# Broadcasts by a repeated column, one-product running maximum, and 30 instead of 24 diagonal taps in a two-block kernel

## The chip, the cores and the metric

The kernel runs as one program on one core of one Trainium2 chip. Its engines are TensorE (PE in the profile; PEld is its weight load), VectorE (DVE), ScalarE (ACT), GpSimd (POOL) and SyncE (SP), which here only issues transfers. The metric is the device time of one execution in microseconds, the median of several.

## The reference

Two decoder blocks run one after the other on 512 tokens of 1024 features, all in float32. Three parts of the reference matter here.

- Every block starts and many end with an RMS norm: a factor per token, `rsqrt(mean(x*x) + eps)`, that multiplies all features of that token.
- The first block's mixer has a stabilised mLSTM. With `b` the running sum of the log forget gates and `i` the input gates, `m` is a running maximum over the tokens, and the weights are `exp(b_t - b_s + i_s - m_t)`. There are four heads and two directions, so eight such units.
- The second block's mixer has a causal depthwise convolution of 31 taps over 512 channels: `cv[t, c] = sum_j w[j, c] * gl[t + j - 30, c] + b[c]`. Behind it stand a layer norm over the channels, a SiLU and an output projection:

```
    gl = glu_a * jax.nn.sigmoid(glu_b)
    cv = causal_dwconv(gl, dw_w) + dw_b
    yb = jax.nn.silu(layernorm(cv, ln_g, ln_b))
    return jnp.concatenate([ya, yb], axis=-1) @ w_out
```

## The kernel before, in words

Activations lie feature-major: 128 features on the partitions, 512 tokens along the row. Weight matrices come in 512 KB pieces (`ws`); ScalarE writes the rounded high part (`wh`, line 208), VectorE the rest (`wl`, line 209), and TensorE makes three products of the float32r type for each pair (lines 237 to 239). An fp32 operand that isn't split goes through TensorE in two passes, which the profile shows as two matmul records for one instruction. The stages follow each other: `mix1` (mLSTM and a gated linear attention), `ffn1`, `pool` (the mixer with the 31 taps), `xa0` (attention to a memory), `ffn2a`, `mla`, `xa1`, `ffn2b`, `final`. Key and value projections of the memory (`mem_kv`) are independent work, which is put between other work as a filler of TensorE.

The order of the instructions on each engine is set when the program is built: the code emits them in program order, with priorities for some, and a list scheduler with its own cost estimates orders each engine's queue. Each queue then runs strictly in that order. `pin` keeps the taps of the convolution in the order in which the code emits them.

Three places matter.

**Per-token factors.** `bcast_cols` (lines 312 to 326) gets a column of 128 factors for each of four token groups and must put them on all partitions as rows. For each group VectorE scales the identity by the column (`dg`, two buffers), and TensorE multiplies ones by that matrix (line 318). ScalarE copies the result out of PSUM as `rb`, or the consumer reads PSUM directly. It is called 13 times.

**Running maximum.** `mx` holds the maxima of the four heads, on partitions 0 to 3 for the forward and 64 to 67 for the backward direction. `ml_build` (one call for each of the eight units) spreads one row of it over all partitions with an fp32 product whose stationary operand is a repeated column of the identity (line 907). ScalarE makes the exponentials from it (line 921) and VectorE multiplies them with the scores (line 926). The PSUM banks in this stage are two each for the tags `mm`, `st`, `nd` and `aux`. The spread maxima lie in `aux`, as do the gate products of the gated linear attention (line 986).

**The 31 taps.** The 512 channels are four groups c of 128. Tap 0 starts the sum `c2` on ScalarE. The other 30 taps of a group are dealt out three ways: `POOLC[c]` taps are products on ScalarE (line 1294, tile `cm`) that GpSimd adds into `c2` (line 1295); `PEC[c]` taps are products of a diagonal matrix, built by ScalarE (line 1272, tile `dgc`), with the shifted rows on TensorE (line 1279), summed in PSUM; VectorE does what is left by a fused multiply and add into the same PSUM bank (line 1303), and then adds both sums as `cv` (line 1307). With `POOLC = (9, 8, 5, 3)` and `PEC = (0, 8, 8, 8)` VectorE has 21, 14, 17 and 19 taps. As each `cv` is ready, TensorE adds it into the mean over the channels (line 1368). `ORDER` lists what the mixer's TensorE work is (`a`, `b` the gated halves, `p` the pooled part, `w` its weights, `k` a piece of `mem_kv`); after each entry eight steps of the tap generator are emitted, and a step is a tap that is not a diagonal one. When the list is done, the rest of the taps and of `mem_kv` alternate. Then come the layer norm's sums (line 1419), the factors, and the output projection.

Of the kernel before, what the change touches and what calls it, by code (L numbers as in the profile page):

```python
# [10 lines left out]
F32 = mybir.dt.float32  # L11
F32R = mybir.dt.float32r
U8 = mybir.dt.uint8
I32 = mybir.dt.int32
ACTF = mybir.ActivationFunctionType
ALU = mybir.AluOpType
# [3 lines left out]
P = 128  # L20
S = 512
# [2 lines left out]
DEC = (3, 6)  # L24
LAG = 0
POOLC = (9, 8, 5, 3)
PEC = (0, 8, 8, 8)
ORDER = 'a1 p3 b2 k a2 p2 k b3 a3 p1 k p0 w3 k w2 w1 w0'
KVS = (0, 2, 0, 1)
TURN = (((2,), (0,)), ((1, 3),))  # L30
# [32 lines left out]
def kernel(ctx: ExitStack, tc: tile.TileContext, A, out, stages=ALL_STAGES):  # L63
    nc = tc.nc
    V, SC, GP, PE, DMA = nc.vector, nc.scalar, nc.gpsimd, nc.tensor, nc.sync
# [20 lines left out]
    def pm(tag="mm", shape=(P, S)):  # L86
        n = used[tag] = used.get(tag, -1) + 1
        b = banks[tag][n % len(banks[tag])]
        return psp.tile(list(shape), F32, tag=f"b{b}", bufs=1, name=tag)

    def ptmp(shape=(P, S), dtype=F32, tag="t", bufs=6):
        return tp.tile(list(shape), dtype, tag=tag, bufs=bufs, name=tag)
# [11 lines left out]
    ident = const.tile([P, P], F32, name="ident")  # L104
    ones = const.tile([P, P], F32, name="ones")
# [71 lines left out]
    def pc(name, i=0):  # L177
        c = base[name] + i
        return par[:, c:c + 1]
# [121 lines left out]
    def rsqrt_mean(src, dim, m):  # L301

        v = col(m)
        V.tensor_scalar(out=v, in0=src, scalar1=1.0 / dim, scalar2=EPS, op0=ALU.mult, op1=ALU.add)
        y, t = col(m), col(m)
        GP.tensor_tensor(out=y, in0=v, in1=mhalf[:, 0:m], op=ALU.pow)
        V.scalar_tensor_tensor(out=t, in0=y, scalar=-0.5, in1=y, op0=ALU.mult, op1=ALU.mult)
        V.tensor_tensor(out=t, in0=t, in1=v, op=ALU.mult)
        V.scalar_tensor_tensor(out=y, in0=t, scalar=1.5, in1=y, op0=ALU.add, op1=ALU.mult)
        return y  # L310

    def bcast_cols(r, m=4, pool=None, stay=False):

        ps = pm("aux", (P, m * P))
        for j in range(m):
            dg = ptmp((P, P), tag="dg", bufs=2)
            V.tensor_scalar(out=dg, in0=ident, scalar1=r[:, j:j + 1], scalar2=None, op0=ALU.mult)
            PE.matmul(ps[:, j * P:(j + 1) * P], lhsT=ones, rhs=dg, start=True, stop=True)  # L318
        if stay:
            return ps  # L320
        if pool is None:
            rb = ptmp((P, m * P), tag="rb", bufs=2)
        else:
            rb = pool.tile([P, m * P], F32, tag="rbp", name="rbp")
        SC.activation(out=rb, in_=ps, func=ACTF.Copy)
        return rb

    class Norm:
# [29 lines left out]
        def finish(self, r=None):  # L358
            if self.g is None:
                return None  # L360
            self.r = self.ss.rstd(D) if r is None else r
            if not self.final:
                self.rb = bcast_cols(self.r)
            return self
# [294 lines left out]
    def mix_heads(mp, layers):  # L659
# [19 lines left out]
        with nc.allow_non_contiguous_dma(reason="a column of 128 for each of 8 feature tiles"):  # L679
            (SC, DMA, GP)[LQ].dma_start(out=par[:, base["mix_pre"]:base["mix_pre"] + KD],  # L680
                         in_=A["norm_mix_pre"].rearrange("o (z p) -> p (o z)", p=P))
# [7 lines left out]
                      in_=wi[:, g0:g0 + 16].rearrange("(k p) c -> p k c", p=P))  # L689
        DMA.dma_start(out=wst[:, :, 16:48],  # L690
                      in_=wi[:, l0:l0 + 32].rearrange("(k p) c -> p k c", p=P))
# [36 lines left out]
        ps = opened[1][0]  # L728
# [6 lines left out]
        def log_sigmoid(dst, x, t):  # L735
# [11 lines left out]

        bt = ptmp()
        um = ptmp()
        mx = mp.tile([P, S], F32, name="mx")  # L750
        GP.memset(um, 0.0)
        GP.memset(mx, 0.0)
        bo = one.to_broadcast([P, S])
# [1 line left out]
                             op0=ALU.mult, op1=ALU.add)  # L755
# [5 lines left out]
                             op0=ALU.mult, op1=ALU.max)  # L761
        V.tensor_tensor_scan(out=mx[64:68, ::-1], data0=bo[32:36], data1=um[32:36, ::-1],
                             initial=0.0, op0=ALU.mult, op1=ALU.max)
        V.tensor_tensor(out=um[64:68], in0=bt[0:4], in1=mx[0:4], op=ALU.add)
        V.tensor_tensor(out=um[96:100], in0=bt[64:68], in1=mx[64:68], op=ALU.add)
        ps = pm("aux")
# [4 lines left out]
        for d in range(2):  # L771
            V.tensor_copy(umc[:, :, 4 * d:4 * d + 4], psv[:, :, 32 * d:32 * d + 4])
            SC.activation(out=em[:, :, 4 * d:4 * d + 4], in_=psv[:, :, 64 + 32 * d:68 + 32 * d],
                          func=ACTF.Exp, scale=-1.0)
# [52 lines left out]
        def w5(nm_, shape=(P, 2, S)):  # L827
            return mp.tile(list(shape), F32, tag="w5", bufs=3, name=nm_)
# [71 lines left out]
        def span(d, j):  # L900
            return (j * P, S) if d == 0 else (0, (j + 1) * P)

        def ml_build(h, d):
            q, k2 = qs[h], khl[h]
            mb = pm("aux")
            r0 = 64 * d + h
            PE.matmul(mb, lhsT=ident[:, r0:r0 + 1].to_broadcast([P, P]), rhs=mx, start=True,
                      stop=True)
            e = w5("e", (P, 1280))
            for js in GRP[d]:  # L910
                st = pm("st")
                o0 = OFF[d][js[0]]
                tot = 0
                for j in js:
                    a, b = span(d, j)
                    o = OFF[d][j] - o0
                    ks = slice(j * P, (j + 1) * P)
                    for i in range(2):
                        PE.matmul(st[:, o:o + b - a], lhsT=k2[:, i, ks], rhs=q[:, a:b],
                                  start=i == 0, stop=i == 1)  # L920
                    SC.activation(out=e[:, OFF[d][j]:OFF[d][j] + b - a], in_=mb[:, a:b],
                                  func=ACTF.Exp, scale=-1.0,
                                  bias=umc[:, j, 4 * d + h:4 * d + h + 1])
                    tot += b - a
                sl = slice(o0, o0 + tot)
                V.tensor_tensor(out=e[:, sl], in0=st[:, :tot], in1=e[:, sl], op=ALU.mult)
                for j in js:
                    a, b = span(d, j)
                    o = OFF[d][j] + (0 if d == 0 else b - a - P)
                    sg = 1 if d == 0 else -1  # L930
                    GP.affine_select(out=e[:, o:o + P], in_=e[:, o:o + P], pattern=[[sg, P]],
                                     compare_op=ALU.is_ge, fill=0.0, base=0,
                                     channel_multiplier=-sg)
            return e
# [300 lines left out]
    def pool_mix(nm, nxt, pp, fill):  # L1235
# [29 lines left out]
        own = {c: {1 + i * 30 // POOLC[c] for i in range(POOLC[c])} for c in range(4)}  # L1265
        dia = {c: [j for j in range(1, 31) if j not in own[c]][:PEC[c]] for c in range(4)}

        def diagonals(c):
            dgs[c] = []
            for j in dia[c]:  # L1270
                dg = pp.tile([P, P], F32, tag="dgc", bufs=10, name="dgc")
                SC.activation(out=dg, in_=ident, func=ACTF.Copy, scale=pc("dw_w", 4 * j + c))
                dgs[c].append(dg)

        def conv_pe(c):
            gl = gls[c]
            cps[c] = pm("cv")
            for n, j in enumerate(dia[c]):
                PE.matmul(cps[c], lhsT=dgs[c][n], rhs=gl[:, j:j + S], start=n == 0,
                          stop=n == PEC[c] - 1)  # L1280

        pin = tc.keep_in_program_order

        def conv(c):
            gl, ps = gls[c], cps[c]
            c2 = pp.tile([P, S], F32, tag="c2", bufs=2, name="c2")
            SC.activation(out=c2, in_=gl[:, 0:S], func=ACTF.Identity, scale=pc("dw_w", c),
                          bias=pc("dw_b", c))
            fresh = not PEC[c]
            for j in range(1, 31):  # L1290
                w = pc("dw_w", 4 * j + c)
                if j in own[c]:
                    t = pp.tile([P, S], F32, tag="cm", bufs=4, name="cm")
                    pin(SC.activation(out=t, in_=gl[:, j:j + S], func=ACTF.Copy, scale=w))
                    pin(GP.tensor_tensor(out=c2, in0=c2, in1=t, op=ALU.add))
                elif j in dia[c]:
                    continue
                elif fresh:
                    V.tensor_scalar(out=ps, in0=gl[:, j:j + S], scalar1=w, scalar2=None,
                                    op0=ALU.mult)  # L1300
                    fresh = False
                else:
                    pin(V.scalar_tensor_tensor(out=ps, in0=gl[:, j:j + S], scalar=w, in1=ps,  # L1303
                                               op0=ALU.mult, op1=ALU.add))
                yield
            cv = pp.tile([P, S], F32, name=f"cv{c}")
            V.tensor_tensor(out=cv, in0=ps, in1=c2, op=ALU.add)
            cvs[c] = cv
            yield
# [104 lines left out]
        for c in range(4):  # L1414
            V.tensor_tensor(out=cvs[c], in0=cvs[c], in1=mean, op=ALU.subtract)
            sq = ptmp(tag="sq", bufs=3)
            SC.activation(out=sq, in_=cvs[c], func=ACTF.Square)
            for j in range(4):
                PE.matmul(pss[:, j:j + 1], lhsT=sq[:, j * P:(j + 1) * P], rhs=ones[:, 0:1],
                          start=c == 0 and j == 0, stop=c == 3 and j == 3)  # L1420
# [10 lines left out]
        r = rsqrt_mean(pss, S, 4)  # L1431
# [3 lines left out]
        for c in range(4):  # L1435
            V.scalar_tensor_tensor(out=cvs[c], in0=cvs[c], scalar=pc("ln_g", c), in1=lb,
                                   op0=ALU.mult, op1=ALU.mult)
# [383 lines left out]
    pcs, pp = ExitStack(), []  # L1821
# [78 lines left out]
```

## Time and profile before

| | |
|---|---|
| median of three runs | 2183.96 us (2183.51 to 2189.16) |
| the profiled execution | 2181.3 us, of which the span of the trace is 2178.9 us |
| mean granted TensorE clock | 0.989 of full speed |
| TensorE busy | 2105.1 us (97%) |
| VectorE busy | 1208.9 us (55%) |
| ScalarE busy | 945.9 us (43%) |
| GpSimd busy | 372.7 us (17%) |

Busy is the share of the span in which an engine executes something. Matmuls overlap each other, so TensorE's work is read from the distance between starts, not from the duration of one. In a row of the timeline the first number is the start in us, the second the duration, and the bracket at the end the idle time of that engine just before, with what ended it. PEclk is the TensorE clock that was granted in a stretch, as a share of full speed (2.4 GHz; the lower level is 1.2 GHz).

### The profile page before, as it was taken

How to read it: one execution, taken by the hardware profiler on the slowest of the kernel's cores; microseconds unless marked ns; L12 is line 12 of the kernel's file. 1: busy time of each engine (PE TensorE's matmuls, PEld its weight loads, DVE VectorE, ACT ScalarE, POOL GpSimd, SP SyncE). 2: the span in 40 equal slices, each digit the busy share in tenths (PEclk: the TensorE clock that was granted, in tenths of full speed). 3: DMA queues.
4: the chain of work that ended last, by engine and by line, in shares of the span. 5: the costliest groups of instructions: out<-in, count | busy, mean ns of one | idle time of the engine just before them, and what ended most of it. 6: DMA issues, size and time to landing. Idle time of an engine off the chain costs nothing.

```text
span 2178.9 us, 27908 instructions
## 1 busy us (share of the span) xinstructions
PE 2105.1 (97%) x10807; PEld 1768.7 (81%) x10807; DVE 1208.9 (55%) x1795; ACT 945.9 (43%) x1561; POOL 372.7 (17%) x414
## 2 busy tenths in 40 slices
PE   7999899999999999899999999999999999999998
PEld 6888778788888876778888888888888888888887
DVE  6655755655532378755665554337885565555432
ACT  5765554433332454343443333226774343333322
POOL 2113411211100047020111110112322011111010
PEclk9999999999999999999999999999999999999999
DMA  5543245233333332532233333331124223333331
GB/s 144 161 152 114 88 145 165 73 102 97 97 112 98 114 102 82 174 118 77 73 92 97 97 97 96 116 107 45 35 93 151 78 58 87 97 97 97 94 102 66
DMA packets 369984, 222.88 MB, mean 102 GB/s; under 512 B 22407, under 2 KB 351036, under 8 KB 369852
## 3 DMA queue, kind: packets, MB, share of 16 engines
q1 hardware_dynamic: 366304, 219.65, 33.9%
q8 instruction: 85, 1.39, 0.3%
q10 hardware_dynamic: 3228, 1.42, 0.2%
q14 instruction: 47, 0.39, 0.1%
q0 software_dynamic: 320, 0.04, 0.0%
HBM read 201.41 MB, written 19.66 MB: 101 GB/s over the span
## 4 chain that ended last, share of the span: by engine, by line
PE 80%; DVE 8%; ACT 5%; issue 3%; POOL 1%; DMA 1%; SPq 0%; ACTq 0%; POOLq 0%; DVEq 0%
PE mm L239 21%; PE mm L237 21%; PE mm L238 21%; PE st L237 2%; PE st L238 2%; PE st L239 2%; PE nd L237 2%; PE nd L238 2%; PE nd L239 1%; DVE wl L209 1%; ACT wh L208 1%; DVE cv L1303 1%; ACT pr L1727 1%; PE aux L318 1%; DVE c L1726 1%
## 5 line engine op out<-in xcount | busy, mean ns | idle before, releaser
L208 ACT ACTIVATE wh<-ws 128x1024 fp32r<-128x1024 f32 (+2 forms) x352 | 361.3, 1029 | 774.1 <-PE mm L239 556.7
L209 DVE TENSOR_TENSOR wl<-ws,wh 128x1024 fp32r<-128x1024 f32 (+2 forms) x352 | 421.9, 1200 | 335.7 <-ACT wh L208 335.4
L237 PE MATMUL mm<-a,wh 128*128 128x512 f32 (+1 forms) x1364 | 530.2, 389 | 2.8 <-ACT a L208 1.3
L239 PE MATMUL mm<-a,wh 128*128 128x512 f32 (+1 forms) x1364 | 528.1, 387 | 1.6 <-DVE a L215 1.6
L238 PE MATMUL mm<-a,wl 128*128 128x512 f32 (+1 forms) x1364 | 527.9, 387 | 0.8 <-DVE wl L209 0.8
L237 PEld LDWEIGHTS mm<-a,wh 128*128 128x128 f32 x1364 | 258.4, 190 | 54.7 <-ACT a L208 1.7
L239 PEld LDWEIGHTS mm<-a,wh 128*128 128x128 f32 x1364 | 258.2, 189 | 54.0 <-DVE a L215 3.4
L238 PEld LDWEIGHTS mm<-a,wl 128*128 128x128 f32 x1364 | 258.3, 189 | 51.6 <-DVE wl L209 2.0
L237 PE MATMUL mm<-hh,wh 128*128 128x512 f32 (+1 forms) x550 | 209.6, 381 | 0.0
L238 PE MATMUL mm<-hh,wl 128*128 128x512 f32 (+1 forms) x550 | 209.3, 381 | 0.0
L239 PE MATMUL mm<-hl,wh 128*128 128x512 f32 (+1 forms) x550 | 209.3, 381 | 0.0
L283 POOL TENSOR_TENSOR sq<-sq 128x512 f32<-128x512 f32 x60 | 92.4, 1540 | 646.6 <-ACT sq L278 562.0
L1203 POOL TENSOR_TENSOR t<-t,rb 128x512 f32<-128x512 f32 x66 | 85.1, 1290 | 613.9 <-ACT t L1202 613.9
L1190 DVE TENSOR_TENSOR t<-mm,rb 128x512 f32<-128x512 f32 x64 | 44.2, 691 | 147.2 <-PE mm L239 147.2
L1206 DVE TENSOR_TENSOR t<-mm,t 128x512 f32<-128x512 f32 x65 | 45.0, 692 | 140.4 <-POOL t L1203 140.4
L239 PEld LDWEIGHTS mm<-hl,wh 128*128 128x128 f32 x550 | 103.4, 188 | 19.8
L238 PEld LDWEIGHTS mm<-hh,wl 128*128 128x128 f32 x550 | 103.4, 188 | 19.7
L237 PEld LDWEIGHTS mm<-hh,wh 128*128 128x128 f32 x550 | 103.4, 188 | 19.6
L237 PE MATMUL mm<-wh,a 128*128 128x256 f32 x346 | 100.1, 290 | 2.3 <-DVE Kl L209 2.3
L239 PE MATMUL mm<-wl,a 128*128 128x256 f32 x346 | 99.6, 288 | 1.8 <-DVE wl L209 1.7
L1199 DVE SCALAR_TENSOR_TENSOR t<-t,par 128x511 f32<-128x511 f32 (+1 forms) x132 | 98.7, 748 | 3.2 <-ACT t L1195 0.9
L1202 ACT ACTIVATE t<-t 128x512 f32<-128x512 f32 x66 | 41.7, 632 | 133.6 <-DVE t L1199 133.5
(469 smaller groups left out, 3553.3 us busy)
## 6 DMA issues: line engine op xcount, KB each, us to landing
ws<-in_ffn_w_up_dram SPq DMA_DIRECT2D x110, 512.0 KB, 3.8
ws<-in_ffn_w_down_dram SPq DMA_DIRECT2D x48, 512.0 KB, 3.8
ws<-in_xa_wkv_dram SPq DMA_DIRECT2D x32, 512.0 KB, 4.4
ws<-in_w_in_dram SPq DMA_DIRECT2D x24, 512.0 KB, 5.0
ws<-in_ffn_w_gate_dram SPq DMA_DIRECT2D x22, 512.0 KB
ws<-in_ffn_w_down_dram SPq DMA_DIRECT2D x24, 384.0 KB, 3.4
ws<-in_xa_wq_dram SPq DMA_DIRECT2D x16, 512.0 KB, 5.5
ws<-in_xa_wo_dram SPq DMA_DIRECT2D x16, 512.0 KB, 3.7
```

Of the source, the lines that this page charges most:

```text
L208: SC.activation(out=hi, in_=src, func=ACTF.Copy)
L209: eng.tensor_tensor(out=lo, in0=src, in1=hi.bitcast(F32), op=ALU.subtract)
L237: PE.matmul(ps, lhsT=lh, rhs=rh, start=start, stop=False)
L238: PE.matmul(ps, lhsT=ll, rhs=rh, start=False, stop=False)
L239: PE.matmul(ps, lhsT=lh, rhs=rl, start=False, stop=stop)
L283: GP.tensor_tensor(out=self.acc, in0=self.acc, in1=self.new, op=ALU.add)
L318: PE.matmul(ps[:, j * P:(j + 1) * P], lhsT=ones, rhs=dg, start=True, stop=True)
L1190: V.tensor_tensor(out=g, in0=pg, in1=rb, op=ALU.mult)
L1199: V.scalar_tensor_tensor(out=cv[:, o], in0=g[:, i], scalar=w, in1=cv[:, o], op0=ALU.mult, op1=ALU.add)
L1202: SC.activation(out=ge, in_=cv, func=func)
L1203: GP.tensor_tensor(out=ge, in0=ge, in1=rb, op=ALU.mult)
L1206: V.tensor_tensor(out=h, in0=pu, in1=ge, op=ALU.mult)
```

## The change

- `bcast_cols` makes no scaled identity any more: the stationary operand of the product is the column of factors itself, repeated 128 times by a step of zero, and the moving operand is the identity. Four VectorE instructions a call go.
- The running maxima are put into a float32r tile `mhl` once: the rounded part on their own partitions, the rest 32 partitions further on. A selecting matrix `sel` (the sum of two columns of the identity) then spreads both with one float32r product for each unit.
- `PEC` is (0, 9, 10, 11): 30 diagonal taps in place of 24, and VectorE has 21, 13, 15 and 16. The ring of diagonals has 11 buffers in place of 10. The tap products between ScalarE and GpSimd go through eight tiles (five `cm` and three of the ring `sq`) in place of four.

```
-PEC = (0, 8, 8, 8)
+PEC = (0, 9, 10, 11)
@@ bcast_cols
         for j in range(m):
-            dg = ptmp((P, P), tag="dg", bufs=2)
-            V.tensor_scalar(out=dg, in0=ident, scalar1=r[:, j:j + 1], scalar2=None, op0=ALU.mult)
-            PE.matmul(ps[:, j * P:(j + 1) * P], lhsT=ones, rhs=dg, start=True, stop=True)
+            PE.matmul(ps[:, j * P:(j + 1) * P], lhsT=r[:, j:j + 1].to_broadcast([P, P]), rhs=ident,
+                      start=True, stop=True)
@@ mix_heads
-        mx = mp.tile([P, S], F32, name="mx")
+        mx = ptmp()
+        mhl = mp.tile([P, S], F32R, name="mx")
+        sel = ptmp((P, P), F32R, tag="dg", bufs=2)
...
+        SC.activation(out=mhl, in_=mx, func=ACTF.Copy)
+        for r0 in (0, 64):
+            V.tensor_tensor(out=mhl[r0 + 32:r0 + 36], in0=mx[r0:r0 + 4],
+                            in1=mhl[r0:r0 + 4].bitcast(F32), op=ALU.subtract)
+        V.tensor_tensor(out=sel[:, 0:96], in0=ident[:, 0:96], in1=ident[:, 32:P], op=ALU.add)
@@ ml_build
-            PE.matmul(mb, lhsT=ident[:, r0:r0 + 1].to_broadcast([P, P]), rhs=mx, start=True,
+            PE.matmul(mb, lhsT=sel[:, r0:r0 + 1].to_broadcast([P, P]), rhs=mhl, start=True,
                       stop=True)
@@ pool_mix
-                dg = pp.tile([P, P], F32, tag="dgc", bufs=10, name="dgc")
+                dg = pp.tile([P, P], F32, tag="dgc", bufs=11, name="dgc")
...
+        def tap_tiles():
+            while True:
+                for n in range(8):
+                    yield ptmp(tag="sq", bufs=3) if n % 3 == 2 or n == 7 else \
+                        pp.tile([P, S], F32, tag="cm", bufs=5, name="cm")
...
-                    t = pp.tile([P, S], F32, tag="cm", bufs=4, name="cm")
+                    t = next(cms)
```

The scheduler places the instructions anew, and the order moves at these places. The lines of the change count from its own code: 1368 of before is 1384 there, 1419 is 1435, 907 is 914, 919 is 926, 943 is 950, 986 is 993, 318 is 316.

First TensorE at the end of the taps, before: the product of the last group's `cv` with ones stands behind the filler (the 256-column products), and ahead of the pooled part's product (`ph`, `pl`) and the layer norm's sums.

```order
L239 MATMUL mm<-wl,a 128x256
L1368 MATMUL aux<-cv_7720,ones 128x512
L237 MATMUL mm<-ph,wh 128x512
L238 MATMUL mm<-ph,wl 128x512
L239 MATMUL mm<-pl,wh 128x512
L1419 MATMUL aux<-ones,sq 128x1 x4
L237 MATMUL mm<-a,wh 128x512
```

The same place of the change:

```order
L237 MATMUL mm<-ph,wh 128x512
L238 MATMUL mm<-ph,wl 128x512
L239 MATMUL mm<-pl,wh 128x512
L1384 MATMUL aux<-cv_7684,ones 128x512
L237 MATMUL mm<-wh,a 128x256
L238 MATMUL mm<-wh,a 128x256
L239 MATMUL mm<-wl,a 128x256
```

48 filler products of 256 columns now stand between the last `cv` and the first sums (line 1435), where before there were three products. In the same way the third group's `cv` now stands ahead of 28 such products that were ahead of it before.

Second TensorE in the mLSTM, at the third head, before: `mx` is spread for a unit, its scores follow (`qs`, `khl`), then `mx` for the next unit, and then 48 filler products (`mhl` here is a memory operand).

```order
L943 MATMUL nd<-v,e 128x130 x2
L907 MATMUL aux<-mx,ident 128x512
L919 MATMUL st<-qs_833,khl 128x512 x2
L919 MATMUL st<-qs_833,khl 128x384 x2
L919 MATMUL st<-qs_833,khl 128x128 x2
L907 MATMUL aux<-mx,ident 128x512
L237 MATMUL nd<-mhl,wh 128x256
L238 MATMUL nd<-mhl,wl 128x256
L239 MATMUL nd<-mhl,wh 128x256
```

The same place of the change (its `mx` is the new float32r tile, `dg` the selecting matrix):

```order
L926 MATMUL st<-qs_831,khl 128x256 x2
L914 MATMUL aux<-mx,dg 128x512 x2
L926 MATMUL st<-qs_831,khl 128x512 x2
L926 MATMUL st<-qs_831,khl 128x384 x2
L926 MATMUL st<-qs_831,khl 128x128 x2
L993 MATMUL aux<-sm,w_333 128x512
L926 MATMUL st<-qs_831,khl 128x256 x2
L237 MATMUL nd<-mhl,wh 128x256
```

A gate product (line 993), which needs an `aux` bank, and the unit's last scores have moved ahead of the 48 filler products.

Third TensorE at the factors in front of the pool stage, before: two products of a scaled identity (`dg`), then filler, then the other two.

```order
L239 MATMUL mm<-a,wh 128x256
L318 MATMUL aux<-dg,ones 128x128 x2
L237 MATMUL mm<-a,wh 128x256
L238 MATMUL mm<-a,wl 128x256
L318 MATMUL aux<-dg,ones 128x128 x2
L239 MATMUL mm<-a,wh 128x256
```

The same place of the change, where the moving operand is `ident` and the repeated column `c` is stationary:

```order
L239 MATMUL mm<-a,wh 128x256
L316 MATMUL aux<-ident,c 128x128 x4
L237 MATMUL mm<-a,wh 128x256
L238 MATMUL mm<-a,wl 128x256
L239 MATMUL mm<-a,wh 128x256
```

The four products stand together where the first pair stood.

## Rows read from the trace of the kernel before

**Rows 1.** The page: busy time, share of the span, instructions of each engine.

```profile
PE 2105.1 (97%) x10807; PEld 1768.7 (81%) x10807; DVE 1208.9 (55%) x1795; ACT 945.9 (43%) x1561; POOL 372.7 (17%) x414
```

**Rows 2.** Waits of TensorE: total us, times, longest us.

```profile
PE aux L318 <- DVE dg L317: 3.5, 6, 1.0
```

**Rows 3.** Stretches of 10 us: length, busy times, granted clock, DMA share, GB/s.

```profile
830.00:840.00 10.00, 6.97 (x13) 2.84 (x12) 9.86 (x14) 4.08 (x9) 6.67 (x8) 0.83 0.32 105
900.00:910.00 10.00, 6.75 (x37) 4.99 (x35) 8.28 (x12) 3.62 (x5) 0.00 (x0) 0.85 0.60 177
910.00:920.00 10.00, 7.21 (x28) 6.02 (x27) 5.42 (x10) 4.86 (x9) 0.00 (x0) 0.67 0.71 236
920.00:930.00 10.00, 9.54 (x52) 7.83 (x50) 3.97 (x12) 2.93 (x4) 1.02 (x1) 0.96 0.38 137
```

**Rows 4.** Timeline of TensorE around the first group of diagonal products.

```profile
802.39 0.39 PE L239 MATMUL mm<-nl,wh 128*128 128x512 f32 x1
802.62 7.03 PE L1279 MATMUL cv<-gl,dgc 128*128 128x512 f32 x16
...
809.72 0.39 PE L238 MATMUL mm<-nh,wl 128*128 128x512 f32 x1
```

**Rows 5.** Tile mx: ns min/median/max, first and last start, forms.

```profile
L907 PEld LDWEIGHTS aux<-mx,ident x16: 187/188/337, 66.6 to 161.3; 128*128 128x128 f32 x16
L907 PE MATMUL aux<-mx,ident x16: 590/591/1061, 66.7 to 161.8; 128*128 128x512 f32 x16
...
L762 DVE TENSOR_TENSOR_SCAN mx<-ones,t x1: 1215/1215/1215, 40.6 to 40.6; 4x512 f32<-4x512 f32 x1
```

**Rows 6.** Tile cv: VectorE's taps.

```profile
L1303 DVE SCALAR_TENSOR_TENSOR cv<-gl,par,cv x70: 740/756/757, 800.8 to 904.5; 128x512 f32<-128x512 f32 x70
```

**Rows 7.** Timeline of TensorE: the waits behind the last tap sums.

```profile
835.44 2.04 PE L1368 MATMUL aux<-cv,ones 128*128 128x512 f32 x2 [3.03 <-DVE cv L1307]
907.02 2.03 PE L1368 MATMUL aux<-cv,ones 128*128 128x512 f32 x2 [3.25 <-DVE cv L1307]
913.12 1.16 PE L1419 MATMUL aux<-ones,sq 128*128 128x1 f32 x8 [2.79 <-ACT sq L1417]
930.86 0.50 PE L237 MATMUL mm<-a,wh 128*128 128x512 f32 x1 [1.32 <-ACT a L208]
```

**Rows 8.** Timeline of ScalarE and VectorE: first group of taps.

```profile
825.42 0.73 ACT L1294 ACTIVATE cm<-gl,par 128x512 f32<-128x512 f32 x1 [0.64 <-POOL c L1295]
...
826.70 0.69 DVE L209 TENSOR_TENSOR pl<-po,ph 128x512 fp32r<-128x512 f32 x1 [2.85 <-ACT ph L208]
```

**Rows 9.** Timeline of VectorE: five taps, a wait for weights, the last sum.

```profile
829.70 3.38 DVE L1303 SCALAR_TENSOR_TENSOR cv<-gl,par,cv 128x512 f32<-128x512 f32 x5
...
845.66 1.23 DVE L209 TENSOR_TENSOR wl<-ws,wh 128x1024 fp32r<-128x1024 f32 x1 [3.70 <-ACT wh L208]
...
906.28 0.68 DVE L1307 TENSOR_TENSOR cv<-cv,c 128x512 f32<-128x512 f32 x1
```

**Rows 10.** Timeline of all engines: the factors in front of the pool stage.

```profile
757.94 0.60 PE L318 MATMUL aux<-dg,ones 128*128 128x128 f32 x4
...
758.36 0.51 DVE L317 TENSOR_SCALAR dg<-ident,c 128x128 f32<-128x128 f32 x2 [0.51 <-PE aux L318]
...
759.45 0.70 DVE L478 TENSOR_TENSOR mm<-a,aux 128x512 f32<-128x512 f32 x1 [0.25 <-PE aux L318]
```

**Rows 11.** Timeline of TensorE: the longest waits behind two post norms.

```profile
390.46 0.50 PE L237 MATMUL op<-a,wh 128*128 128x512 f32 x1 [1.56 <-ACT a L214]
...
769.79 0.50 PE L237 MATMUL op<-nh,wh 128*128 128x512 f32 x1 [1.48 <-ACT nh L214]
```

**Rows 12.** Timeline of TensorE and ScalarE in the mLSTM, third head.

```profile
139.50 0.80 PE L919 MATMUL st<-qs,khl 128*128 128x256 f32 x2 [2.63 <-DVE e L926]
...
143.59 1.07 PE L907 MATMUL aux<-mx,ident 128*128 128x512 f32 x2
...
144.39 0.48 ACT L921 ACTIVATE e<-aux,umc 128x256 f32<-128x256 f32 x1
```

More of the change, by code (lines that the diff above doesn't have):

```diff
@@ L1282, in pool_mix @@
         pin = tc.keep_in_program_order
+        def tap_tiles():
[3 more added lines that the diff above has]
+                        pp.tile([P, S], F32, tag="cm", bufs=5, name="cm")
+        cms = tap_tiles()
         def conv(c):
```

## Prediction

> **What bounds the kernel now.** I read the page's busy shares first, then TensorE's waits, then the stretches of 10 us, and last the timelines of the engines around the places that the change touches. TensorE is busy for 97% of the span and no other engine for more than 55% [rows 1], so an instruction taken from TensorE is worth its full length nearly everywhere, and one taken from another engine only where TensorE waits for it. The sum is made against the profiled execution, 2181.3 us; the median of the runs is 2.7 us more, which I add at the end. The one long stage where TensorE does wait is the mixer with the 31 taps, from about 800 to 940. There it stands 3.03, 3.25, 2.79 and 1.32 us [rows 7], together 10.4 us, and behind each of the longer waits the granted clock falls: 0.83 in one stretch of 10 us, then 0.85, 0.67 and 0.96 [rows 3]. The missing 0.17, 0.15, 0.33 and 0.04 of 10 us each are 6.9 us of TensorE's time at full speed. So the stage loses 17.3 us to waits and what follows them, and this is the largest thing that the change can win back.
>
> The granted clock comes back to 1.00 in the stretches that follow, when products run again without a gap. The Trainium skill, "TensorE: Matmul & The Clock Gate", Part 1 (The HAM clock gate), says that the throttled state is the default and that activity is what releases it; the rows agree. [...]
>
> **Units.** A float32r product of 512 columns starts 0.23 us after the one before (802.39 to 802.62). Eight diagonal products, 16 records in fp32, lie between 802.62 and the next product at 809.72; less one step of 0.23 and divided by eight, one takes 0.86 us [rows 4]. The fp32 spread of the running maximum is of the same form, 512 columns in two records of 590 ns, and I take it at 0.86 as well [rows 5].
>
> **The running maximum.** Eight spreads go from 0.86 to 0.23: −5.0 us of TensorE. Added are one ScalarE copy, two VectorE subtractions on four partitions and one small addition. The second scan starts at 40.6 and takes 1.2, and the first spread starts at 66.7 [rows 5], so these have some 25 us of cover and I take them at nothing; without that cover they would be some 2 us of one chain. The weight load of a repeated column is not slower: 188 ns for it [rows 5]. What goes against it is the new order. A gate product (986, now 993) has moved ahead of 48 fillers, and it needs the `aux` bank that the unit's exponentials read. In the trace of before the exponentials of the second spread's predecessor start their last piece at 144.39 and take 0.48, so the bank is free at about 144.9, while TensorE comes past the spread at about 143.2 (143.59, less the 0.63 saved on it, and one step of 0.23) [rows 12]. That is a new wait of 1.7 us at a place where the clock is not safe: TensorE has just stood 2.63 at 139.50 [rows 12]. Behind the waiting product lie the last scores and the fillers, all of which wait with it. If the clock falls as in the first stretch of [rows 3] it costs another 1.7. From 0 to 4 us, I take 2.5, nearer to the wait plus part of the clock. The term is −2.5; its ends are −5.0 and −1.0, and +1 if the other units' waits grow too.
>
> **The broadcasts.** TensorE keeps its four products a call with the same two passes; 52 VectorE instructions go. VectorE is busy 55% [rows 1], so these are worth nothing in themselves; what counts is the chain. In front of the pool stage the first pair of products starts at 757.94, the second pair of `dg` waits for it until 758.36 and takes 0.51, and the consumer starts at 759.45 [rows 10]. With all four products together (0.60 for a pair) the consumer would start some 0.5 sooner, and half of 0.51 for the first `dg` goes too: about 0.8 to 0.9 a call. It reaches TensorE where TensorE waits on the far end of the chain, as behind two post norms, which stand 1.56 and 1.48 [rows 11]: −1.8 together. TensorE also waits six times for a `dg` itself, 3.5 us in all [rows 2]. What it waited for is then the column, one instruction (half of 0.51) sooner: six times 0.26, −1.6. The term is −3.4; its ends are −7 (all of both kinds of waits) and 0 (the column is late by as much as before).
>
> **The taps.** Six more diagonals cost TensorE 6 × 0.86 = +5.2 us. VectorE loses six taps; one lasts 756 ns [rows 6], but in a row of five they take 3.38, so 0.67 each [rows 9]: −4.0 us. The eight tiles let ScalarE run further ahead of GpSimd. Before, it stood 0.64 for GpSimd at 825.42, and the rounding of the pooled part, queued behind its tap products, kept VectorE waiting 2.85 at 826.70 [rows 8]. I expect that wait to go, since ScalarE then needs no tile back at that point.
>
> What then becomes late, wait by wait:
> First `cv`. VectorE delivered it for 835.44; without the 2.85 that is 832.6, while TensorE arrives at 832.4 (835.44 − 3.03) plus one diagonal more of 0.86 [rows 7]. The 3.03 goes, and with it the 1.7 of the clock behind it.
> Second and third `cv`: no wait of note before, and TensorE comes later (one and three more diagonals). The third is moved ahead of 28 fillers of 256 columns, 0.12 each (half of 0.23), thus 3.4 us, about what the diagonals add by then. I take nothing.
> Fourth `cv`. It was ready with the sum that starts at 906.28 and lasts 0.68 [rows 9], at 906.96. VectorE has 4.0 less to do, and its own waits for weights, such as 3.70 at 845.66 [rows 9], end earlier by some 2, because TensorE frees the weights 4.7 sooner less the diagonals done by then: ready at about 900.9. TensorE came to it at 903.8 (907.02 − 3.25 [rows 7]). It now comes 4.7 earlier from the first wait, 5.8 earlier since 48 fillers stand behind it, and 5.2 later for the diagonals: 898.5. So a wait of about 2.5 stays, with 1.7 of clock.
> The sums of the layer norm. The wait of 2.79 goes: the 48 fillers, 5.8 us, now cover the centring and squaring of the last group, for which there were three products before. The last wait of 1.32 for the normalised operand has no such cover; it stays, with 0.5 of clock.
> So 6.0 of the 17.3 stay: 5.2 + 6.0 − 17.3 = −6.1. The ends: all of the waits go, −12.1; none of them goes, +5.2.
>
> The `mla` stage changes its order by a few rows. I see no long wait there that it touches; 0, with 2 us either way.
>
> **Sum.** −2.5 − 3.4 − 6.1 = −12.0, thus 2169.3 for a profiled execution and 2172 for the median. The ends of the terms do not all come together: −24 would be 2160, and the upper ends (+1, 0, +5.2) about 2190.
>
> **The rivals.**
> The pool stage runs clean. The fourth `cv` too is in time, because VectorE gains more than I allow, and the clock stays up: −12.1 from that term, and −4.5 from the two others less their new wait. For it: VectorE's wait for weights of 3.70 shows that it is held by TensorE in part. Against: it is busy 9.86 of 10 us at 830 [rows 3], and the product was moved forward by 5.8. Sum −18 or so: 2166, down to 2160.
> Only the first two edits pay. The waits at the first and the last `cv` come back at other places because the fillers have been moved behind them, and the gain in waits equals the 5.2 of the diagonals: −2.5 − 3.4 = −6 and a little clock: 2179. For it: VectorE has 65 taps still, and work for the weights between them in the order of its queue. Against: the 2.79 is covered by 5.8 of fillers.
> VectorE is paced by TensorE. In the order of its queue VectorE holds the low parts of weights between the taps, and these come when TensorE has freed the piece before: the 3.70 at 845.66. Each diagonal put ahead of such a release moves VectorE by 0.86. If this decides from the second group on, the fourth `cv` comes as late as before plus 5.2 − 4.0, TensorE reaches it 5.8 sooner, and the wait becomes 3.25 + 5.8 with more clock lost: the stage is 5.2 + some 4 worse, and against −6 that is +3, or 2187. It decides from the point at which VectorE's waits for weights exceed the 4.0 saved. For it: that one wait alone is nearly the 4.0. Against: TensorE runs 4.7 ahead once the first wait has gone.
>
> **How the numbers follow.** A change below 0.3%, 6.5 us, can't be told from none here. I give the forecast (2166 to 2177) 0.50, the clean stage 0.20, the two edits alone 0.20, the slower case 0.10. Faster by over 0.3%, below 2177.4: nearly all of the first two and half of the third, 0.78. Slower, over 2190.5: a third or so of the last and little else, 0.05. Within: 0.17. The range of 2160 to 2183 leaves out part of the last rival and a little at the bottom; the forecast's own is 2166 to 2177.
>
> **What would show it.** In the profile after: eight records of the spread, not 16, each with about 0.23 to the next start; a wait of some 1.7 ahead of the gate product (993) near 143; waits for `dg` gone at 316 and the two behind post norms down to about 0.7; at the `cv` products (1384) no wait at the first, 2 to 3 at the last; none at the layer norm's sums (1435); and a granted clock of 1.00 from 830 to 840 and over 0.8 from 900 to 930. It is wrong if the first `cv` still waits, if the fourth waits over 5, or if a wait for GpSimd's sum takes VectorE's place.

## The result and the profile after

The changed kernel took 2168.36 us (median of six runs, 2164.08 to 2173.21), the kernel before 2187.72 us beside it; the ratio is 0.9915, with a 95% interval of 0.9898 to 0.9932. It is faster by 15 to 22 us, where 12.0 were forecast. The time lies inside the range; a later comparison of the same two kernels (e5) gave 0.9920 (0.9903 to 0.9938). The profiled execution of the change has a span of 2166.4 us, 12.5 less than before.

The page's busy times, in answer to [rows 1]:

```profile
PE 2097.3 (97%) x10811; PEld 1767.8 (82%) x10811; DVE 1195.9 (55%) x1740; ACT 948.5 (44%) x1568; POOL 375.8 (17%) x414
```

VectorE lost 55 records (of 52 scaled identities and six taps gone, and three instructions come). The list of TensorE's waits (total us, times, longest us), in answer to [rows 2]:

```profile
PE st L1098 <- DVE xb L1087: 5.5, 2, 3.9
PE st L503 <- DVE x L480: 3.8, 1, 3.8
PE mm L237 <- DVE t L209: 3.4, 1, 3.4
...
PE aux L316 <- DVE c L309: 2.4, 4, 0.9
...
PE op L237 <- ACT nh L214: 1.5, 1, 1.5
...
PE aux L1384 <- DVE cv L1323: 1.4, 1, 1.4
...
PE op L237 <- ACT a L214: 0.7, 1, 0.7
...
PE aux L993 <- ACT e L928: 0.6, 1, 0.6
```

No wait at the layer norm's sums (1435) is left, the one at the first `cv` (1384) is 1.4, and the wait of 993 is small. Of the waits behind the two post norms [rows 11] one is down to 0.7 and the other stays at 1.5. New are 3.4 for a `t` and 3.8 for an `x` (0.8 before), both VectorE's. The 3.9 for an `xb` was 1.6 before; the run of the change again takes that up. The mixer with the taps, in answer to [rows 3] and [rows 7], first in stretches of 10 us (length, busy times of TensorE, its weight load, VectorE, ScalarE, GpSimd, then granted clock, DMA share, GB/s):

```profile
820.00:830.00 10.00, 8.62 (x31) 5.44 (x30) 10.00 (x12) 4.86 (x9) 9.68 (x6) 1.00 0.25 82
830.00:840.00 10.00, 10.00 (x45) 6.50 (x44) 6.02 (x10) 4.21 (x10) 6.23 (x9) 1.00 0.16 52
890.00:900.00 10.00, 6.58 (x32) 5.07 (x31) 7.88 (x11) 4.77 (x7) 0.00 (x0) 0.73 0.54 171
900.00:910.00 10.00, 10.00 (x76) 9.74 (x76) 6.48 (x10) 5.58 (x10) 0.00 (x0) 0.93 0.52 161
```

and TensorE's timeline:

```profile
829.61 1.10 PE L1384 MATMUL aux<-cv,ones 128*128 128x512 f32 x2 [1.38 <-DVE cv L1323]
...
892.30 0.28 PE L239 MATMUL mm<-wl,a 128*128 128x256 f32 x1
896.00 0.76 PE L237 MATMUL mm<-ph,wh 128*128 128x512 f32 x1 [3.42 <-DVE t L209]
...
919.88 0.50 PE L237 MATMUL mm<-a,wh 128*128 128x512 f32 x1 [1.10 <-ACT a L208]
```

The clock stays at 1.00 behind the first `cv`; there is one loss left, 2.7 and 0.7 us at 0.73 and 0.93 behind the wait of 3.42. The waits and the clock of the stage took 17.3 us before. Now it is 1.38 + 3.42 + 1.10 + 3.4 = 9.3, where 6.0 had been forecast.

The spread maxima, in answer to [rows 5]:

```profile
L914 PE MATMUL aux<-mx,dg x8: 388/395/478, 64.8 to 153.4; 128*128 128x512 f32 x8
```

Eight records instead of 16, and the last starts 8.4 us sooner than that of before.

**A ledger.** To tell work from waits I split each profiled span in three: TensorE's idle time; the clock's part, which is half of the time in which TensorE executed at the lower level; and the rest, TensorE's work at full speed. Each number is worked out from that kernel's trace.

| kernel | span | idle | clock | work |
|---|---|---|---|---|
| before | 2178.9 | 73.8 | 21.5 | 2083.5 |
| the change | 2166.4 | 69.1 | 18.5 | 2078.8 |
| the change, other profile (e5) | 2170.8 | 70.5 | 21.6 | 2078.7 |
| maximum only (e1) | 2174.6 | 71.7 | 25.1 | 2077.8 |
| columns only (e2) | 2179.4 | 75.9 | 23.4 | 2080.0 |
| taps only (e3) | 2169.4 | 67.2 | 14.6 | 2087.6 |
| taps, four tiles (e4) | 2176.4 | 71.2 | 18.0 | 2087.1 |
| no more diagonals (e6) | 2173.8 | 73.9 | 23.9 | 2076.0 |
| one old factor (e7) | 2165.7 | 69.3 | 15.3 | 2081.0 |
| the same, more for GpSimd (e8) | 2167.9 | 68.4 | 20.8 | 2078.7 |
| change without columns (e9) | 2170.6 | 70.0 | 18.9 | 2081.7 |
| change without maximum (e10) | 2172.9 | 70.8 | 15.5 | 2086.6 |
| change without taps (e11) | 2175.4 | 74.5 | 25.9 | 2075.0 |
| eight tiles only (e12) | 2184.9 | 72.9 | 27.6 | 2084.4 |

The work column repeats best: 2078.8 and 2078.7 for the change, and 2083.5 and 2084.4 for before and e12, in which TensorE's order is the same from start to end. But e7 and e8, with the same order up to the last `cv` and the same products behind it, are 2.3 apart, so a difference of 2 in the whole work tells little. The 4.8, 5.3 and 10 us of work in the expectations of e9, e10 and e11 come from a coarser split, which counted the lowered clock also where TensorE stood idle; by this one they are 3.5, 5.7 and 8.5. Between the two profiles of the change lie 4.4 us, of which 3.1 are clock and 1.4 idle time. The same stretch in both, the change and then its second profile:

```profile
120.00:140.00 20.00, 16.95 (x113) 14.60 (x114) 14.13 (x34) 18.44 (x41) 3.12 (x13) 1.00 0.59 168
```

```profile
120.00:140.00 20.00, 17.25 (x104) 14.45 (x102) 14.16 (x34) 18.01 (x37) 3.61 (x10) 0.86 0.58 165
```

TensorE stands some 3 us in both, and its clock fell in one only. So the span of one profile can't settle a term of 2 us, and the timed ratios are needed beside it.

### The profile page after: what moved, and what is told of

Same layout as the page of the kernel before. It is cut to its first block, busy times and chain, and to the rows that moved or that the text cites. A ratio compares the mean times of both kernels' runs of the same rounds, so it can differ in the third digit from the quotient of the medians.

```text
span 2166.4 us, 27873 instructions
## 1 busy us (share of the span) xinstructions
PE 2097.3 (97%) x10811; PEld 1767.8 (82%) x10811; DVE 1195.9 (55%) x1740; ACT 948.5 (44%) x1568; POOL 375.8 (17%) x414
## 4 chain that ended last, share of the span: by engine, by line
PE 83%; DVE 7%; ACT 5%; issue 3%; POOL 1%; DMA 0%; SPq 0%; ACTq 0%; POOLq 0%; DVEq 0%
PE mm L237 22%; PE mm L239 22%; PE mm L238 22%; PE st L237 2%; PE st L238 2%; PE st L239 2%; PE nd L237 2%; PE nd L238 1%; PE nd L239 1%; DVE wl L209 1%; PE cv L1286 1%; ACT pr L1743 1%; ACT wh L208 1%; PE nd L1118 1%; PE aux L316 1%
```

## The experiments

Times against before are ratios times 2185 us. e1 to e4 ran on one chip, e5 to e8 on a second and e9 to e12 on a third, each against before on the same chip.

**One part at a time.** e1 has `mhl`, `sel` and the product of the maximum alone, e2 the repeated column alone, e3 the taps alone; e9, e10 and e11 are the change with that same part put back.

```
e1  -  lhsT=ident[:, r0:r0 + 1]..., rhs=mx     +  lhsT=sel[:, r0:r0 + 1]..., rhs=mhl
e2  -  lhsT=ones, rhs=dg                       +  lhsT=r[:, j:j + 1].to_broadcast([P, P]), rhs=ident
e3  -  PEC = (0, 8, 8, 8)                      +  PEC = (0, 9, 10, 11)
    -  bufs=10 / t = pp.tile(tag="cm", bufs=4) +  bufs=11 / t = next(cms)
```

> The kernel before with the running maximum's edit alone (rounded tile, selecting matrix, one float32r product a unit). Theory: eight spreads at 0.63 us less are -5.0 us, of which a wait for the bank at the gate product that moved ahead of 48 fillers takes some, so -1 to -4 us, about -2.5. Rival A: the gate product waits under 1 us and nothing is lost, -5 us. Rival B: the gain up to about 180 us is handed back in the gated linear attention, where TensorE waits for VectorE's xb, about 0 to -1 us.

> The kernel before with the repeated column in the broadcasts alone. Theory: -3.4 us: TensorE's six waits for the scaled identity fall from 3.5 to about 2 us and the two waits behind post norms from 1.5 to about 0.7 each. Rival: the column of factors, not the scaled identity, is what comes late, and other engines take up the slack, so TensorE waits as long: 0 us, inside what the runs can tell.

> The kernel before with 30 diagonal taps, the ring of 11 and the eight tap tiles, and the old broadcasts and maximum. Theory: -6 us (5.2 more for the diagonals, 11 less of waits and clock): no wait at the first cv, 1 to 3 us at the last, none at the layer norm's sums. Rival: VectorE is paced by TensorE and the waits come back, 0 to +3 us, with a wait of over 4 us at the last cv.

> The change with the scaled identity in the broadcasts as before. The profiles so far put the repeated column at 4.8 us less work of TensorE and as much more in waits and lowered clock (VectorE's first sum x behind the first mixer above all), so theory: worth 0 to 3 us, this kernel -13 to -17 us against before. Rival: the four edits add up as measured singly (maximum -2, taps -7): -10 us, and the column is worth 7.

> The change with the fp32 spread of the running maximum as before. Theory: the spread is 5.3 us of TensorE's work and its new waits are below 1 us, so this kernel is 4 to 5 us slower than the change, -12 to -14 us against before. Rival: as measured singly, worth 2 us: -15 us.

> Maximum and columns as in the change, the mixer with the 31 taps as before. Theory: 10 us less work of TensorE, 3 to 5 handed back to waits, -5 to -7 us against before, with the waits of 3.0, 3.2 and 2.8 us in the mixer as before. Rival: as measured singly, -2 to -3 us.

| | ratio to before (95%) | us | | ratio to before (95%) | us |
|---|---|---|---|---|---|
| maximum only | 0.9990 (0.9976 to 1.0004) | −2.2 | change without it | 0.9959 (0.9945 to 0.9974) | −9.0 |
| columns only | 0.9998 (0.9986 to 1.0010) | −0.4 | change without them | 0.9951 (0.9934 to 0.9968) | −10.7 |
| taps only | 0.9966 (0.9949 to 0.9982) | −7.4 | change without them | 0.9974 (0.9962 to 0.9987) | −5.7 |

The single parts add up to −10.0, the change itself is at −17.5 (e5). Taken out of it, a part is worth more than alone: 8.5 for the maximum, 6.8 for the columns, 11.8 for the taps, 27 in all. Each ratio is known to 3 us or so. A plain sum fits all seven within that, or nearly (least squares: 3.9, 2.1 and 8.1, together 14.1, against 17.5 with an interval from 13.5 to 21.2). So that the parts help each other isn't shown. The taps are the largest by every one of these readings, and the columns alone gain nothing that can be told.

The numbers of e1 and e3 are the theory's. In e1's trace no wait at the gate product is left to speak of, which is rival A's mechanism; its −5 lies at the edge of the interval. In e3 the first `cv` waited 1.4 and not 0, and 3.4 stood ahead of the last, as in the change. e2's rival held, though for another reason than the one it gives: the work fell by 3.5 us (ledger), and 2.1 more of waits with 1.9 more of clock took it back. In e2's list of waits stands

```profile
PE st L503 <- DVE x L480: 4.4, 1, 4.4
```

The 4.4 is new, against at most 1.4 in every kernel with the scaled identity at that call. The `xb` wait is 2.3 longer in e2 too, but that one varies between executions (below). e9 came out at its rival's number, the columns worth some 7 in company, though its interval (−7.0 to −14.4 us) takes in the theory's −13 as well. e10, −5.7 to −12.0 us, is slower than both of its numbers. The 8.5 that the maximum is worth there are hardly told from the 2.2 of e1, and they are no more than its work there, which is 7.8 by the ledger; why it is 7.8 and not the 5.7 of e1 is open, with 2 of scatter. e11's theory held, with the mixer's waits as before (7.0 us for `cv` in 3, 2.8 for `sq`).

**Where the work of the columns went.** I had costed their products at nothing. The timeline of TensorE in front of the pool stage, in e9 (scaled identity) and then in the change:

```profile
755.46 0.28 PE L239 MATMUL mm<-a,wh 128*128 128x256 f32 x1
755.58 0.60 PE L318 MATMUL aux<-dg,ones 128*128 128x128 f32 x4
755.94 0.36 PE L237 MATMUL mm<-a,wh 128*128 128x256 f32 x1
756.14 0.28 PE L238 MATMUL mm<-a,wl 128*128 128x256 f32 x1
756.34 0.71 PE L318 MATMUL aux<-dg,ones 128*128 128x128 f32 x4
756.81 0.36 PE L239 MATMUL mm<-a,wh 128*128 128x256 f32 x1
757.01 0.28 PE L237 MATMUL mm<-a,wh 128*128 128x256 f32 x1
```

```profile
753.80 0.28 PE L239 MATMUL mm<-a,wh 128*128 128x256 f32 x1
753.92 1.05 PE L316 MATMUL aux<-ident,c 128*128 128x128 f32 x8
754.72 0.36 PE L237 MATMUL mm<-a,wh 128*128 128x256 f32 x1
754.92 0.28 PE L238 MATMUL mm<-a,wl 128*128 128x256 f32 x1
```

From 755.46 to 757.01 there are four fillers of 0.12 and the two pairs, so the pairs cost 1.07; from 753.80 to 754.92 two fillers and all four products, which cost 0.88. Behind each group the next filler takes 0.20 to the next start in place of 0.12, and the second group begins 0.08 late. That is 0.2 a call here. Every one of the 13 calls was cut in two or three and stands in one group now. From the first diagonal product on, the eight calls there save 1.3 of work both times, from before to e2 (1330.8 to 1329.5) and from e9 to the change (1335.1 to 1333.8), 0.16 a call. So the 13 calls make an estimated 2.1 to 2.5 of the 2.9 us (e9 against the change) or 3.5 us (e2 against before); what is left lies within the scatter.

**One old factor.** The wait of 3.8 for `x` is behind the first mixer. VectorE and TensorE in the change:

```profile
369.10 2.35 DVE L209 TENSOR_TENSOR wl<-ws,wh 128x1024 fp32r<-128x1024 f32 x2
371.37 0.42 DVE L209 TENSOR_TENSOR ko<-st,ko 128x256 fp32r<-128x256 f32 x1
371.71 0.68 DVE L480 TENSOR_TENSOR x<-z,st 128x512 f32<-128x512 f32 x1
```

```profile
367.57 1.04 PE L503 MATMUL st<-ident,xs 128*128 128x128 f32 x8
372.44 2.40 PE L503 MATMUL st<-ident,xs 128*128 128x128 f32 x10 [3.83 <-DVE x L480]
```

Two roundings of weights and a memory piece stand ahead of the first `x`, which frees TensorE's bank; before, one rounding stood there. With the old form at this call VectorE's order here is that of before:

```
-            rb = bcast_cols(r, stay=True)
+            rb = bcast_cols(r, stay=True, old=bool(xs))   # old: lhsT=ones, rhs=dg
```

> The change, but the factors behind the first mixer (the one call that reads the input again) are spread by the scaled identity as before. Theory: the repeated column there put VectorE's first sum x behind one more rounding of weights and a memory piece, and TensorE's transposes wait 3.8 us for it instead of 0.8; with the old form the wait is about 0.8 again, with 1.7 us less of lowered clock, and the call itself is 0.3 us longer: 3 to 5 us faster than the change. Rival: the wait comes back behind the transposes as waits of TensorE for the normalised operand (1.0 and 1.6 before): no gain, within 1 us.

```profile
PE op L237 <- ACT a L214: 2.2, 2, 1.6
...
PE st L508 <- DVE x L485: 1.3, 1, 1.3
```

The wait for `x` fell to 1.3 as the theory has it, but that behind the post norm came back at 1.6, as the rival has it. The work is 2.2 higher (ledger), but not so in e8, which has the same call. The ratio is 0.9919 (0.9901 to 0.9937), the change's own beside it 0.9920: no gain.

**The tiles and the diagonals.** e4 is e3 with four tiles, e12 the eight tiles alone, e6 the change with `PEC = (0, 8, 8, 8)` and ten buffers.

> As the taps alone, but ScalarE and GpSimd pass the products through four tiles as before (30 diagonal taps and the ring of 11 stay). Theory: ScalarE again stands for GpSimd's sum, VectorE waits some 2.5 us for the rounded pooled part, TensorE waits about 2 us at the first cv with the clock lowered after it: about 3 to 4 us slower than the taps with eight tiles, so -2 us against the kernel before. Rival: the number of tiles is without effect, since VectorE has a tap less in the second group and more time elsewhere: as the taps alone, -6 us.

> The kernel before with the eight tap tiles alone, 24 diagonals. Theory: the wait at the first cv falls from 3.0 to about 1.4 and the clock behind it stays up, 2 to 3 us in all; the waits at the last cv and the layer norm's sums stay at 3.2 and 2.8: -2 to -3 us. Rival: ScalarE running ahead delays the roundings that VectorE waits for: 0 to +2 us.

> The change with 24 diagonal taps as before (eight tiles, columns and maximum stay). Theory: TensorE saves 4 to 5 us of diagonals and pays them back at the last cv and the layer norm's sums, where before stood 3.2 and 2.8 us with 5 us of clock: 3 to 6 us slower than the change. Rival: the eight tiles alone bring the gain of the stage and the diagonals are a zero sum: as the change, within 2 us.

e4: 0.9976 (0.9962 to 0.9990), −5.2 us, 2 behind e3, which the intervals don't separate. Its trace does. VectorE, then TensorE:

```profile
828.01 0.69 DVE L209 TENSOR_TENSOR pl<-po,ph 128x512 fp32r<-128x512 f32 x1 [2.84 <-ACT ph L208]
```

```profile
836.75 1.10 PE L1368 MATMUL aux<-cv,ones 128*128 128x512 f32 x2 [3.03 <-DVE cv L1307]
```

These are the waits of before within 0.01 [rows 7, 8], so the ninth diagonal does nothing for the first `cv`; the tiles alone take the first of the two waits away and bring the second down to 1.38. The clock behind the wait of 3.03 stayed at 1.00 in e4's profile, where it was 0.83 before: the wait came without its clock. e12 shows the other side, the first wait at 1.38 and the later ones unchanged:

```profile
PE st L1091 <- DVE xb L1080: 5.5, 2, 3.9
PE aux L1377 <- DVE cv L1316: 5.4, 3, 3.2
...
PE aux L1428 <- ACT sq L1426: 2.8, 1, 2.8
```

Its time is 0.9992 (0.9979 to 1.0006): −1.7 us, near the theory's −2 to −3 but not told from none. e6: 0.9940 (0.9923 to 0.9956), 4.4 us behind the change beside it, inside the theory's 3 to 6, though the two intervals overlap. It has the waits of 3.2 and 2.8 at the last `cv` and the sums again. What it saves repeats: from the first diagonal product to the end TensorE's work is 1329.4 in e6 and 1333.8 in the change, 1330.6 in e12 and 1335.1 in e3. So six diagonals cost 4.4 us there, and with the fillers that moved behind the products they bring back more than that.

Which part of the gain is larger, the tiles' or the diagonals', isn't shown. Put into the kernel before, the tiles bring 1.7 (e12) and the diagonals 5.2 (e4). With columns and maximum in place, the tiles bring 7.4 (from e11 at −5.7 to e6 at −13.1, whose intervals don't meet) and the diagonals 4.4 more.

**Three taps more for GpSimd.** GpSimd does nothing from 890 on, and the wait of 3.42 looked like VectorE's taps. e8 is e7 with `POOLC = (9, 8, 5, 6)`.

> As the one with the old factor, and three more taps of the last group go to ScalarE and GpSimd, which sits idle then (POOLC of 6 for the last group, VectorE 13 taps). Theory: VectorE's bank release ahead of the pooled product comes 3 x 0.67 = 2 us sooner, so TensorE's wait of 3.4 falls to about 1.4 and with it some clock: 2 to 4 us faster than with the old factor alone. Rival: ScalarE's three more products delay the roundings that VectorE waits for, or GpSimd's sum comes late: 0 to +2 us.

0.9929 (0.9914 to 0.9945), 2 us behind e7, which the intervals don't separate: the theory fell, and the rival's time came, but not for its reason. ScalarE and VectorE in e7, and then VectorE in e8:

```profile
893.03 1.06 ACT L208 ACTIVATE wh<-ws 128x1024 fp32r<-128x1024 f32 x1 [0.38 <-PE mm L238]
```

```profile
894.12 1.23 DVE L209 TENSOR_TENSOR wl<-ws,wh 128x1024 fp32r<-128x1024 f32 x1 [0.21 <-ACT wh L208]
895.26 0.75 DVE L1324 SCALAR_TENSOR_TENSOR cv<-gl,par,cv 128x512 f32<-128x512 f32 x1
895.92 0.42 DVE L209 TENSOR_TENSOR t<-mm,t 128x256 fp32r<-128x256 f32 x1
896.25 0.68 DVE L1328 TENSOR_TENSOR cv<-cv,c 128x512 f32<-128x512 f32 x1
```

```profile
894.12 1.23 DVE L209 TENSOR_TENSOR wl<-ws,wh 128x1024 fp32r<-128x1024 f32 x1 [0.21 <-ACT wh L208]
895.27 0.68 DVE L1328 TENSOR_TENSOR cv<-cv,c 128x512 f32<-128x512 f32 x1
895.87 0.41 DVE L209 TENSOR_TENSOR t<-mm,t 128x256 fp32r<-128x256 f32 x1
```

What holds `t` and `cv` there is the rounding of weights ahead of them, which waits for ScalarE's `wh`, and ScalarE for the buffer that TensorE frees. The rounding starts at 894.12 in both. VectorE is paced by TensorE at this point, as a rival in the prediction had it; three taps less let `cv` start 1.0 sooner and `t` 0.05. TensorE's wait was 2.94 for `cv`, which now stands first, in place of 3.42 for `t`.

**The change again.**

> The changed kernel once more, beside the variants below. Theory: the time differs by a few us between runs of one kernel because TensorE's clock falls or doesn't behind a wait (1.7 us for a stretch of 10 us at 0.83), above all at VectorE's xb near 260, where one profile of an unchanged order waited 1.6 and another 3.8. So -14 to -19 us against before, and waits at the same places, but the xb wait and its clock may be absent. Rival: the xb wait belongs to the changed order and stands again at 3.8 us.

0.9920 (0.9903 to 0.9938), as the theory has it. But the wait of 3.9 for `xb` stood there again. It is no child of the changed order either: in e12 it is 3.9 (above), and e12's order is that of before on every engine up to the pool stage, hundreds of us later. e3, with the same order there, has the short one:

```profile
PE st L1091 <- DVE xb L1080: 3.0, 2, 1.6
```

Of the 14 profiles three show 1.6 (before, e1, e3), nine 3.8 or 3.9, two 4.7. It varies between executions; what decides it stays open.

## Why the prediction was right, by its steps

- **What bounds the kernel.** Right. The stage with the taps is the largest gain (7.4 alone, 11.8 out of the whole), and TensorE's work and its waits explain the rest.
- **The running maximum, −2.5.** The mechanism was right, the size too small: the work fell by 5.7 us (5.0 said), and the feared wait at the gate product was 0.6, not 1.7 with 1.7 of clock. Timed, it was −2.2 alone, with an interval that takes in both −2.5 and −5.0, and 8.5 out of the whole; so the size isn't settled by the times.
- **The broadcasts, −3.4.** Two mistakes that nearly cancel. That TensorE keeps its passes and so its time was wrong: 2.9 to 3.5 us less work. That the shorter chain pays at the post norms held for one of two waits (1.56 to 0.7; 1.48 stayed 1.5), and the waits for `dg`, 3.5, became 2.4 for the column, 1.1 less rather than 1.6. The new order of VectorE made the wait at `x` 3.8 in place of 0.8, which I had not priced: I looked at the order of TensorE alone there.
- **The taps, −6.1.** Right, by −7.4 (−3.9 to −11.1). The unit of 0.86 holds: the first group takes 7.32 us for nine products and 6.46 for eight. The stage's work rose by 4.4 rather than 5.2; where the rest went I did not find. The sums' wait of 2.79 went, the last fell from 1.32 to 1.10. The last `cv` was named as a wait of 2.5 with 1.7 of clock; 3.42 with 3.4 stood one split product ahead of it, for a bank, and `cv` was ready right behind.
- **The first `cv`.** That it still waits was one of the prediction's own signs of being wrong, and it kept 1.38 of its 3.03. VectorE's wait of 2.85 went, but VectorE gained only 0.9 (`cv` starts 32.0 us after the first diagonal product before, 834.62 less 802.62, and 31.1 now, 828.79 less 797.69). Of the missing 2.0, 1.1 are in one rounding of weights, shown in the last section. The other 0.8 is TensorE's: VectorE's `t` waits for a product that stands behind the first group of diagonals, of which there is one more. Before, 12.55 us behind the first diagonal product, and now, 13.37 behind it:

```profile
815.17 0.69 DVE L1251 TENSOR_TENSOR t<-mm,rb 128x512 f32<-128x512 f32 x1 [4.51 <-PE mm L239]
```

```profile
811.06 0.69 DVE L1258 TENSOR_TENSOR t<-mm,rb 128x512 f32<-128x512 f32 x1 [4.39 <-PE mm L239]
```

  The two parts come apart in the experiments: `cv` starts 32.8 behind the first diagonal product in e4 (ninth diagonal, four tiles) and 30.3 in e12 (eight diagonals, eight tiles). That is the rival of VectorE paced by TensorE, at the first group too; the prediction took VectorE to be free there.
- **The sum and the base.** The profiled spans differ by 12.5, against 12.0 forecast, but that they agree is luck. The forecast was made of +0.2 of work (−5.0 and +5.2) and −12.2 of waits and clock; the ledger shows −4.7 of work, −4.7 of waits and −3.0 of clock. The runs differ by 17 to 19. Of that, 3.7 come from the base: the median of before was 2187.7 beside the change and 2184.0 in the runs that I had added the sum to. The change itself ran at 2168.4 where 2172 was forecast.
- **The rivals.** In the clean stage, −12.1 and −4.5 don't make −18 but −16.6; with the forecast's own −5.9 for the other two terms it is −18. The timed gain came near that number, but the stage did not run clean: the mixer kept 9.3 us of waits and clock.

## What to carry to other kernels

Price an edit of a scheduled kernel in two ledgers, the bottleneck's work and its waits: here the work terms (−5.7 and −7.8 for the maximum, −3.5 and −2.9 for the columns, +4.4 for the diagonals) came out alike within some 2 us, while the waits moved to other places and, with the clock, varied by 4.5 us between two executions of one kernel. When instructions are taken from an engine, look at its own new order too, for what now stands ahead of the instruction that frees the bottleneck's bank. A wait that ends on a busy engine isn't shortened by less work there if what it works on comes from the bottleneck.

## What the runs showed of the hardware

VectorE's rounding of a weight piece, `wl<-ws,wh`, and GpSimd's additions of the taps stop each other: the one that starts second waits for the other. In the change, VectorE and then GpSimd:

```profile
821.63 2.30 DVE L209 TENSOR_TENSOR wl<-ws,wh 128x1024 fp32r<-128x1024 f32 x1
```

```profile
821.56 1.28 POOL L1311 TENSOR_TENSOR c<-c,cm 128x512 f32<-128x512 f32 x1
```

and the same rounding in the kernel before, VectorE and then GpSimd:

```profile
828.57 1.22 DVE L209 TENSOR_TENSOR wl<-ws,wh 128x1024 fp32r<-128x1024 f32 x1
```

```profile
828.63 2.28 POOL L1295 TENSOR_TENSOR c<-c,cm 128x512 f32<-128x512 f32 x1
```

In the change the addition was 0.07 us ahead. It took its 1.28, and the rounding ended 1.09 after it, so 2.30 after its own start. In the kernel before the rounding was 0.06 ahead, took 1.22, and the addition was drawn out to 2.28. In all 15 overlaps of the two in these two traces the second ended 1.08 to 1.16 us after the first. The Trainium skill, "Trainium Architecture — The Big Picture", What this means for kernel authors, says that within the engines' side of SBUF VectorE and GpSimd contend for a shared port pair, as an exclusive lock and not a split; the trace agrees, with the 1.08 to 1.16 us. Here 0.13 us of order decide over 1.1 us on VectorE, on the way to the first `cv`.

A group of small fp32 products was dearer when it was cut in two among float32r ones: 1.07 against 0.88 us for four. The operands differ as well, but the products themselves cost the same, 0.36 and 0.47 us to the next start for the two pairs against 0.80 for the four; the difference lies at the edges of the groups.
